# Gate and up products of a hybrid block: partial sums kept in PSUM banks and read out midway

## The chip, the cores and the metric

One core of a Trainium2 chip runs the whole kernel. The metric is device time in microseconds (us); the figure for the kernel before is the median of three runs. TensorE (PE in the rows) multiplies into PSUM, which has eight banks of 128 partitions by 512 float32 values here; VectorE (DVE), ScalarE (ACT) and GpSimd (POOL) work beside it, and SyncE (SP) issues the DMAs. Each engine takes its instructions strictly in the order in which they stand, and waits on semaphores for the others.

## What is computed

One layer on 2048 tokens of width 1024 in float32: a norm, an input projection, two mixers (gated linear attention and spatial gating), an output projection, then the feed-forward part with 2816 hidden columns, and a final norm. The change touches the two products `a` and `bu` of the feed-forward part alone:

```python
n2 = rms_norm(h, norm2_w[l])
a = jnp.einsum('btd,df->btf', n2, w_ffn_gate[l])
bu = jnp.einsum('btd,df->btf', n2, w_ffn_up[l])
h = h + jnp.einsum('btf,fd->btd', jax.nn.silu(a) * bu, w_ffn_down[l])
```

## The kernel before

The tokens go through in two halves of 1024 (`for s in range(2)`), each half as two blocks of 512. The gate and up products (`gate_up`) treat a half as 2 x 2 blocks: two blocks of tokens, two halves of D, two column tiles of 128. Winograd's form of Strassen's scheme makes the four result blocks of a pair of column tiles from seven block products instead of eight. There are 11 pairs in a half (i = 0 to 10), each with one `Weights` object for gate and then one for up: 22 objects, 154 block products per half. Pair 0 goes alternately between gate and up, since its token operands are still being made; from pair 1 on gate's seven products come first and then up's.

A block product m takes a weight operand `op` and a token operand `t1` to `t7`. Both are split into a high and a low part (`split`: ScalarE casts the high part, line 94, VectorE subtracts it for the low part, line 95), and `mm3` multiplies low by high, high by low and high by high: 3 matmuls for each of 4 tiles of K, so 12 of 128x512 a product, lines 114 to 116. `prep` makes the weight operands, seven products ahead (`AHEAD`), with sums of weight blocks by VectorE (`sw`, line 634).

Before, every product has a PSUM bank of its own (`o = ps()`; eight banks go round). The sums are made outside: products 1, 5 and 7 are copied out by ScalarE (line 659), and VectorE adds everything up, with eight additions for a `Weights` object: line 662 once, 666 once, 669 once, 672 once, and the one in `put_gate` (line 686) or `put_up` (line 692) four times. `put_gate` then applies Silu in place in the tile `cg` (line 687). `put_up` multiplies up's block into `cg` (line 693) and writes three of the four blocks to DRAM (`ad`, line 696). After the last block four more VectorE rows make the sums `cs` (lines 700 to 703) that the down-projection needs, which go to DRAM too (704, 705).

The tiles `cg`, `cs` and the 14 token operands all come from one pool of 16 buffers (`big`). So in gate and up two buffers are left for `cg` and `cs`, and a pair's `cg` lies where the `cg` of the pair before it lay: it can be written only after VectorE has read the old one for `cs` and after the three writes of line 696 have landed.

A scheduler sets the order in which each engine's instructions stand. The names below are tiles with the number that the build gave them; they differ between the two kernels only where the change made other tiles.

Of the kernel before, what the change touches and what calls it, by code (L numbers as in the profile page):

```python
# [15 lines left out]
P = 128  # L16
# [17 lines left out]
def hybrid_block(ctx, tc, x, norm1_w, w_in, w_gate_up, b_gate_up, gla_norm_w, sg_ln_w, sg_ln_b,  # L34
# [15 lines left out]
    def ps():  # L50
        return psp.tile([P, 512], F32, name="ps", tag="ps")
# [11 lines left out]
    # A generator emits one step at a time; tick() runs a step of each after a weight tile's products.  # L63
# [28 lines left out]
    def split(hi, lo, src):  # L92
        """hi + lo == src, each with 12 significant bits."""
        nc.scalar.copy(hi, src)  # L94
        nc.vector.tensor_tensor(lo, src, f32(hi), ALU.subtract)  # L95
# [5 lines left out]
    def load_w(srcs, a, b):  # L101
        """srcs: DRAM views [P, a, ...], side by side; the two parts of [P, a, b] in SBUF."""
        raw = view(rawp, F32, "raw", a, b)
        o = 0
        for s in srcs:
            nc.sync.dma_start(raw[:, :, o:o + s.shape[2]], s)
            o += s.shape[2]
        hi, lo = view(wp, F32R, "whi", a, b), view(wp, F32R, "wlo", a, b)
        split(hi, lo, raw)
        return hi, lo  # L110

    def mm3(o, l, r, first, last):
        (lh, ll), (rh, rl) = l, r
        nc.tensor.matmul(o, lhsT=ll, rhs=rh, start=first, stop=False)  # L114
        nc.tensor.matmul(o, lhsT=lh, rhs=rl, start=False, stop=False)  # L115
        nc.tensor.matmul(o, lhsT=lh, rhs=rh, start=False, stop=last)  # L116

    def rsq(dst, ss, n, k):
        """dst = 1 / sqrt(ss / n + eps)"""
        nc.vector.tensor_scalar(dst, ss, 1.0 / n, EPS, ALU.mult, ALU.add)  # L120
        nc.gpsimd.tensor_tensor(dst, dst, half[:, :k], ALU.pow)
# [8 lines left out]
    class Act:  # L130
        """A transposed operand: nk row tiles of 128 by 512 tokens, two parts."""
# [10 lines left out]
        def row(self, k, n=1):  # L142
            """Row tiles k .. k+n-1, for all tokens."""
            s = slice(k % 4, k % 4 + n)
            return self.hi[k // 4][:, s, :], self.lo[k // 4][:, s, :]

        def put(self, i, t, src):
            """Row tiles 4i .. 4i+3 of token tile t from PSUM."""
            s = slice(t * P, (t + 1) * P)
            split(self.hi[i][:, :, s], self.lo[i][:, :, s], src.rearrange("p (a b) -> p a b", b=P))  # L150

    def row_tiles(u):
        """Two units as four row tiles of D."""
        return [u[t // 2].rearrange("p a b -> p (a b)")[:, (t % 2) * D:(t % 2 + 1) * D] for t in range(TT)]
# [36 lines left out]
    def tok_group(w, col_list, act, ks=2, order=None, outer=None, done=None, before=None, ws=None, hook=None, pre=None):  # L191
        """Token-major product: four PSUM tiles [128 tokens, n]."""
        n = sum(c for _, c in col_list)
        order = order or list(range(0, act.nk, ks))
        acc = [None] * TT

        def load(k0):
            return tok_load(w, col_list, k0, min(ks, act.nk - k0))

        def products(t, k0, hi, lo):  # L200
            if acc[t] is None:
                acc[t] = ps()
            for j in range(hi.shape[1]):
                mm3(acc[t][:, :n], act(k0 + j, t * P, (t + 1) * P), (hi[:, j, :], lo[:, j, :]),
                    k0 == order[0] and j == 0, k0 == order[-1] and j == hi.shape[1] - 1)

        if outer:
            ws = ws or [load(k0) for k0 in order]
            for ts in outer:
                for k0, (hi, lo) in zip(order, ws):  # L210
                    if hook:
                        hook(ts[-1], k0)
                    for t in ts:
                        products(t, k0, hi, lo)
                for t in ts:
                    done(t, acc[t])
                tick()
        else:
            for k0 in order:
                if before and k0 in before:  # L220
                    finish(before[k0])
                hi, lo = pre.pop(k0) if pre and k0 in pre else load(k0)
                for t in range(TT):
                    products(t, k0, hi, lo)
                    if k0 == order[-1]:
                        done(t, acc[t])
                tick()
# [4 lines left out]
    def col_pair(ws, act, a=0, b=NB):  # L232
        """Transposed product: two PSUM tiles [128 columns, tokens a..b]."""
        acc = [ps(), ps()]
        for i, (hi, lo) in enumerate(ws):
            for k in range(4):
                for c in range(2):
                    cs = slice(c * P, (c + 1) * P)
                    mm3(acc[c][:, :b - a], (hi[:, k, cs], lo[:, k, cs]), act(4 * i + k, a, b), i + k == 0, i == 1 and k == 3)
            tick()  # L240
        return acc
# [15 lines left out]
    # 0 where a chunk starts, 1 elsewhere: the prefix scan's carry  # L257
# [3 lines left out]
    # keep[j, i] = 1 where j <= i, in both halves of the rows  # L261
# [12 lines left out]
    # the decay's up-projection: rows hi, hi, lo against the low-rank input's hi, lo, hi  # L274
# [9 lines left out]
    def constants():  # L284
# [9 lines left out]
        # spatial gating: masked, transposed weights and the two biases  # L294
# [27 lines left out]
    def down_sums():  # L322
        """The four sums of blocks of w_d that the down-projection takes, to DRAM."""
# [18 lines left out]
    def mix(blk, nT, first_w):  # L342
        """Both mixers of one block; the transposed operand of the output projection."""
# [59 lines left out]
        # The two factors of a head's output: its queries and scores, its state and values. Of the 128 rows,  # L403
        # the head's own half (as its keys lie) holds the former, the other half the latter.
# [3 lines left out]
        def right(n):  # L408
            """[rows, head in pair, pair, DV] of chunk n"""
            return rights[n % 2][:, n // 2]  # L410
# [169 lines left out]
    def project(blk, hx, mixT, g_att, pre, put, outer, ahead=None):  # L580
        """Output projection, residual, norm 2."""
# [28 lines left out]
    # Blocks: column tile c, half of D, half of the tokens. An operand m is the m-th factor's two parts.  # L610
    ORDER = (1, 2, 5, 7, 6, 3, 4)
    AHEAD = 6

    class Weights:
        """One pair of column tiles of w, as seven operands; put(c, l, in0, in1, tmp) takes a result's two addends."""

        def __init__(self, w, c0, act, put, tmp, unit=False):
# [9 lines left out]
            self.act, self.put, self.tmp, self.op, self.t = act, put, tmp, {}, {}  # L627

# [21 lines left out]

        def mul(self, m):
            o = ps()
# [22 lines left out]
    def gate_up(s, act):  # L675
        def matrices(i):
            unit = []

# [5 lines left out]
            def put_gate(c, l, x, y, tmp):  # L684
                g = part(2 * c + l)
                nc.vector.tensor_tensor(g, x, y, ALU.add)
                nc.scalar.activation(g, g, AF.Silu)

            def put_up(c, l, x, y, tmp):
                g = part(2 * c + l)  # L690
                u = tpt("u") if tmp is None else tmp
                nc.vector.tensor_tensor(u, x, y, ALU.add)
# [4 lines left out]
                if (c, l) == (1, 0):  # L697
# [12 lines left out]
            def tmp_up(m):  # L710
                return tpt(f"p{m}")

            return [lambda: Weights(w_g, 2 * i * P, act, put_gate, tmp_gate),
                    lambda: Weights(w_u, 2 * i * P, act, put_up, tmp_up, i == 0)]

        seq = []
        for i in range(NF // 2):
            mats = matrices(i)
            if i == 0:
                seq += [(2 * i + j, mats[j], m) for m in ORDER for j in range(2)]  # L720
            else:
                seq += [(2 * i + j, mats[j], m) for j in range(2) for m in ORDER]
# [3 lines left out]
        def ahead(n):  # L726
            """Operands up to the n-th product."""
# [7 lines left out]
        def run(late):  # L735
            for at, (key, _, m) in enumerate(seq):
# [9 lines left out]
    # Blocks: half of the tokens, column tile of a pair, half of D.  # L746
# [129 lines left out]
    for s in range(2):  # L876
# [118 lines left out]
```

## Time and profile before

| | us |
|---|---|
| median of three runs | 2015.6 (2015.26 to 2017.57) |
| span of the profiled execution | 2014.3 |
| TensorE busy | 1987.2 (99%) |
| VectorE busy | 1422.5 (71%) |
| ScalarE busy | 858.8 (43%) |

The span is 1.3 us under the median; what lies around the span of the profiled execution is not listed. Gate and up lie at about 382 to 803 us in the first half and at 1375 to 1796 us in the second, some 421 us each. Mean clock of TensorE over the span: 0.998 of full speed. A matmul's row gives 389 ns, but matmuls overlap: the starts of two that follow each other are 0.227 us apart, which is what counts.

### The profile page before, as it was taken

The numbers are of one execution on the slowest core, as the hardware profiler recorded it, in microseconds if no ns is written. First come the engines' busy times: TensorE is split into PE (matmuls) and PEld (weight loads), VectorE is DVE, ScalarE is ACT, GpSimd is POOL, SyncE is SP. The second block draws the span as 40 slices with busy tenths as digits, with TensorE's granted clock in tenths as the row PEclk, the third lists the DMA queues.
The fourth block names the chain that finished last, engine by engine and source line by source line (L and its number), as shares of the span: only waits on it lengthen the run. The fifth ranks groups of instructions, "written<-read, shape, count | busy, mean of one in ns | idle before, by whom it ended". The sixth has DMA issues, their size and how long they took to land. (4 is left out here: it accounts for less than half of the span.)

```text
span 2014.3 us, 26324 instructions
## 1 busy us (share of the span) xinstructions
PE 1987.2 (99%) x9909; PEld 1659.1 (82%) x9909; DVE 1422.5 (71%) x2397; ACT 858.8 (43%) x1418; POOL 80.8 (4%) x102
## 2 busy tenths in 40 slices
PE   7999999999999999999999999999999999999998
PEld 6888888878888888888888888887888888888886
DVE  5676776798777777555776655658977877775466
ACT  4534635453333333433562535346433333334334
POOL 1011000000000000000100100100000000000000
PEclk9999999999999999999999999999999999999999
DMA  5646664323323324865754344323332332367555
GB/s 192 188 168 222 228 200 167 115 94 105 115 95 102 118 95 145 290 200 185 242 178 105 115 143 144 103 84 116 114 111 95 106 114 95 104 208 268 188 164 197
DMA packets 189790, 303.05 MB, mean 150 GB/s; under 512 B 14503, under 2 KB 93021, under 8 KB 188638
## 3 DMA queue, kind: packets, MB, share of 16 engines
q1 hardware_dynamic: 189662, 301.36, 45.2%
q8 instruction: 78, 1.28, 0.3%
q14 instruction: 50, 0.41, 0.1%
HBM read 224.25 MB, written 72.88 MB: 148 GB/s over the span
## 5 line engine op out<-in xcount | busy, mean ns | idle before, releaser
L94 ACT CAST whi<-raw 128x1024 fp32r<-128x1024 f32 (+3 forms) x191 | 192.0, 1006 | 403.3 <-PE ps L115 208.5
L95 DVE TENSOR_TENSOR wlo<-raw,whi 128x1024 fp32r<-128x1024 f32 (+3 forms) x191 | 221.9, 1168 | 150.1 <-ACT whi L94 144.1
L114 PE MATMUL ps<-whi,aop 128*128 128x512 f32 x552 | 215.1, 390 | 0.0
L116 PE MATMUL ps<-whi,aop 128*128 128x512 f32 x552 | 214.8, 389 | 0.0
L115 PE MATMUL ps<-wlo,aop 128*128 128x512 f32 x552 | 214.8, 389 | 0.0
L94 ACT CAST op<-sw 128x512 fp32r<-128x512 f32 x176 | 107.5, 621 | 184.5 <-DVE sw L634 159.6
L114 PE MATMUL ps<-whi,nTl 128*128 128x512 f32 (+2 forms) x512 | 177.4, 346 | 3.4 <-DVE nTl L95 3.4
L116 PE MATMUL ps<-whi,nTh 128*128 128x512 f32 (+2 forms) x512 | 174.4, 341 | 0.0
L115 PE MATMUL ps<-wlo,nTh 128*128 128x512 f32 (+2 forms) x512 | 174.3, 340 | 0.0
L95 DVE TENSOR_TENSOR aop<-raw,aop 128x1024 fp32r<-128x1024 f32 x84 | 95.3, 1135 | 97.5 <-ACT aop L94 97.3
L95 DVE TENSOR_TENSOR op<-sw,op 128x512 fp32r<-128x512 f32 x176 | 121.5, 692 | 43.0 <-ACT op L94 42.6
L94 ACT CAST aop<-raw 128x1024 fp32r<-128x1024 f32 x84 | 82.0, 979 | 136.6 <-DMA raw<-ad 135.1
L116 PEld LDWEIGHTS ps<-whi,aop 128*128 128x128 f32 x552 | 103.6, 188 | 21.6
L115 PEld LDWEIGHTS ps<-wlo,aop 128*128 128x128 f32 x552 | 103.6, 188 | 21.4
L114 PEld LDWEIGHTS ps<-whi,aop 128*128 128x128 f32 x552 | 103.6, 188 | 21.4
L659 ACT COPY p<-ps 128x512 f32<-128x512 f32 x88 | 51.5, 588 | 149.2 <-PE ps L116 143.6
L95 DVE TENSOR_TENSOR op<-raw,op 128x512 fp32r<-128x512 f32 x132 | 89.3, 693 | 31.0 <-ACT op L94 30.5
L114 PEld LDWEIGHTS ps<-whi,nTl 128*128 128x128 f32 x512 | 98.1, 192 | 14.5 <-ACT whi L94 3.5
L116 PEld LDWEIGHTS ps<-whi,nTh 128*128 128x128 f32 x512 | 98.1, 192 | 10.2
L115 PEld LDWEIGHTS ps<-wlo,nTh 128*128 128x128 f32 x512 | 98.2, 192 | 9.4
L114 PE MATMUL ps<-whi,mixTl 128*128 128x512 f32 x256 | 101.9, 398 | 1.4 <-DVE mixTl L95 1.2
L114 PE MATMUL ps<-nTh,wlo 128*128 128x512 f32 x256 | 101.8, 398 | 0.0
(229 smaller groups left out, 4712.4 us busy)
## 6 DMA issues: line engine op xcount, KB each, us to landing
raw<-in_w_in_dram SPq DMA_DIRECT2D x72, 512.0 KB, 3.9
raw<-ad SPq DMA_DIRECT2D x70, 512.0 KB, 3.9
raw<-in_w_ffn_gate_dram SPq DMA_DIRECT2D x44, 512.0 KB, 3.6
raw<-in_w_ffn_up_dram SPq DMA_DIRECT2D x44, 512.0 KB, 3.6
raw<-td SPq DMA_DIRECT2D x40, 512.0 KB, 3.9
ad<-cg SPq DMA_DIRECT2D x66, 256.0 KB, 2.0
ad<-cs SPq DMA_DIRECT2D x22, 768.0 KB, 3.6
raw<-in_w_out_dram SPq DMA_DIRECT2D x32, 512.0 KB, 3.8
```

Of the source, the lines that this page charges most:

```text
L94: nc.scalar.copy(hi, src)
L95: nc.vector.tensor_tensor(lo, src, f32(hi), ALU.subtract)
L114: nc.tensor.matmul(o, lhsT=ll, rhs=rh, start=first, stop=False)
L115: nc.tensor.matmul(o, lhsT=lh, rhs=rl, start=False, stop=False)
L116: nc.tensor.matmul(o, lhsT=lh, rhs=rh, start=False, stop=last)
L659: nc.scalar.copy(t[m], o)
```

## The change

For the pairs 1 to 10 (`if i:`) `Weights` gets a function `keep`, and `mul` goes to the new `mul_kept`. An object then takes three banks instead of seven: products 1, 6, 5 and 3 are added up in the first, 7 and 4 in the second, 2 has the third (`BANK`). A product that is not the first in its bank starts without clearing it. The products go in the order 1, 2, 6, 7, 5, 4, 3 (`MULTIPLIED`), their operands are made in the order 1, 2, 5, 6, 7, 4, 3 (`PREPARED`). The bank's running sum is read in the middle: ScalarE copies it after products 1, 6 and 7; VectorE reads it after 5 and after 4 and adds one of the copies; after 3 it is the result block (0, 1) as it stands. Of the eight additions three are left. Gate's copies go straight into `cg` (parts 0, 2, 3), and gate's block (0, 1) goes from PSUM through Silu into `cg`. Block (1, 0) is now written out before (0, 1), and `cs` follows (0, 1). Pair 0 is left as it was.

```diff
-        nc.tensor.matmul(o, lhsT=ll, rhs=rh, start=first, stop=False)
+        nc.tensor.matmul(o, lhsT=ll, rhs=rh, start=first, stop=False, skip_group_check=shared)
...
+    PREPARED, MULTIPLIED = (1, 2, 5, 6, 7, 4, 3), (1, 2, 6, 7, 5, 4, 3)
+    BANK = {1: 0, 6: 0, 5: 0, 3: 0, 7: 1, 4: 1, 2: 2}
...
+        def mul_kept(self, m):
+            key = BANK[m]
+            first = key not in self.acc
+            if first:
+                self.acc[key] = ps()
+            o = self.acc[key]
+            (wh, wl), (th, tl) = self.op.pop(m), self.act[m]
+            for k in range(4):
+                mm3(o, (wh[:, k], wl[:, k]), (th[:, k], tl[:, k]), first and k == 0, k == 3, True)
+            t = self.t
+            if m in (1, 6, 7):
+                t[m] = self.keep(m)
+                nc.scalar.copy(t[m], o)
+            elif m == 3:
+                self.put(0, 1, o, None, None)
+            else:
+                c, l, other = {2: (0, 0, 1), 5: (1, 1, 7), 4: (1, 0, 6)}[m]
+                self.put(c, l, o, t[other], t[other])
...
             def put_gate(c, l, x, y, tmp):
                 g = part(2 * c + l)
+                if y is None:
+                    nc.scalar.activation(g, x, AF.Silu)
+                    return
...
-                if (c, l) == (1, 0):
+                left.discard((c, l))
+                if not left:
                     cs = bigt(F32, "cs")
...
+            if i:
+                def keep_gate(m):
+                    return part({1: 0, 6: 2, 7: 3}[m])
+
+                def keep_up(m):
+                    return tpt(f"p{m}")
...
-                seq += [(2 * i + j, mats[j], m) for j in range(2) for m in ORDER]
+                seq += [(2 * i + j, mats[j], m) for j in range(2) for m in PREPARED]
+                muls += [(2 * i + j, m) for j in range(2) for m in MULTIPLIED]
```

TensorE, the gate products of pair 1 in the first half. Before, the first row of each product; `ps_` is its bank's tile, `t1h` the token operand, and the semaphore named after "waits" belongs to VectorE (DVE) or ScalarE (Activation):

```order
L114 MATMUL ps_3963<-t1h_3308,op_3831 128x512 [waits DVE_49]
...
L114 MATMUL ps_3985<-t2h_3352,op_3850 128x512 [waits DVE_49]
...
L114 MATMUL ps_4004<-t5h_3495,op_3872 128x512 [waits DVE_49]
...
L114 MATMUL ps_4023<-t7h_3663,op_3893 128x512 [waits DVE_49]
...
L114 MATMUL ps_4043<-t6h_3697,op_3913 128x512 [waits DVE_49]
```

In the change, at the same place:

```order
L115 MATMUL ps_3963<-t1h_3308,op_3831 128x512 [waits DVE_49]
...
L115 MATMUL ps_3985<-t2h_3352,op_3850 128x512 [waits DVE_49]
...
L115 MATMUL ps_4021<-t7h_3663,op_3913 128x512 [waits DVE_49]
...
L115 MATMUL ps_3963<-t6h_3697,op_3892 128x512 [waits Activation_49]
...
L115 MATMUL ps_4021<-t4h_3760,op_3932 128x512 [waits DVE_49,Activation_49]
...
L115 MATMUL ps_3963<-t5h_3495,op_3872 128x512 [waits Activation_49]
...
L115 MATMUL ps_3963<-t3h_3728,op_3960 128x512 [waits DVE_49]
```

Here the scheduler has put 7 ahead of 6, and 5 after the first four matmuls of 4; in the other 19 objects of a half the order is that of `MULTIPLIED`. Product 6 comes back to the bank of product 1 and waits for ScalarE's copy out of it, product 5 for the copy after 6.

ScalarE at the same place. Before, from the casts of up's operands to the first copy into pair 1's `cg` (`cg_3998`); DMAHW is a DMA queue's semaphore:

```order
L687 ACTIVATE cg_3690<-cg_3690 128x512 [waits DVE_49]
L94 CAST op_3982<-raw_3978 128x512 [waits DMAHW6_49,Activation_49]
L94 CAST op_4001<-raw_3979 128x512 [waits DMAHW0_49,Activation_49]
L659 COPY cg_3998<-ps_4004 128x512 [waits DMAHW5_49,DMAHW1_49,DMAHW7_49,DVE_49,PE_49]
L659 COPY cg_3998<-ps_4023 128x512 [waits PE_49]
```

In the change, where pair 1's `cg` is `cg_3976`:

```order
L718 ACTIVATE cg_3690<-cg_3690 128x512 [waits DVE_49]
L94 CAST op_3960<-sw_3870 128x512 [waits DVE_49,PE_49,Activation_49]
L94 CAST op_3982<-raw_3978 128x512 [waits DMAHW6_49,PE_49,Activation_49]
L669 COPY cg_3976<-ps_3963 128x512 [waits DMAHW5_49,DMAHW7_49,DMAHW1_49,PE_49]
L94 CAST op_4000<-raw_3979 128x512 [waits DMAHW0_49,Activation_49]
L94 CAST op_4018<-sw_4016 128x512 [waits DVE_49,PE_49,Activation_49]
L669 COPY cg_3976<-ps_4021 128x512 [waits PE_49]
L718 ACTIVATE cg_3976<-cg_3976 128x512 [waits DVE_49]
L94 CAST op_4036<-sw_4016 128x512 [waits DVE_49,Activation_49]
L669 COPY cg_3976<-ps_3963 128x512 [waits PE_49]
```

The first copy into the new `cg` was that of product 5 and is now that of product 1; it waits for the same three writes of pair 0's `cg`.

VectorE at the turn from a later pair to the next. Before, from up's last product (`ps_4518`, product 4) on:

```order
L672 TENSOR_TENSOR p7_4468<-p7_4468,ps_4518 128x512 [waits PE_49]
L700 TENSOR_TENSOR cs_4535<-cg_4289 128x512 [waits DMAHW4_49,DMAHW3_49,DVE_49]
...
L701 TENSOR_TENSOR cs_4535<-cs_4535,cg_4289 128x512 [waits DVE_49]
...
L702 TENSOR_TENSOR cs_4535<-cg_4289 128x512
L703 TENSOR_TENSOR cs_4535<-cg_4289,cs_4535 128x512 [waits DVE_49]
```

In the change, from up's product 4 (`ps_4422`) over its last, 3 (`ps_4362`), to the first addition of the next gate:

```order
L726 TENSOR_TENSOR p6_4415<-ps_4422,p6_4415 128x512 [waits PE_49]
L95 TENSOR_TENSOR op_4500<-sw_4417,op_4500 128x512 [waits Activation_49]
L727 TENSOR_TENSOR cg_4246<-p6_4415,cg_4246 128x512 [waits DVE_49]
L727 TENSOR_TENSOR cg_4246<-ps_4362,cg_4246 128x512 [waits PE_49]
L95 TENSOR_TENSOR op_4522<-raw_4518,op_4522 128x512 [waits Activation_49]
L735 TENSOR_TENSOR cs_4492<-cg_4246 128x512 [waits DMAHW5_49,DMAHW4_49,DVE_49]
L737 TENSOR_TENSOR cs_4492<-cg_4246 128x512
L736 TENSOR_TENSOR cs_4492<-cs_4492,cg_4246 128x512 [waits DVE_49]
L738 TENSOR_TENSOR cs_4492<-cg_4246,cs_4492 128x512 [waits DVE_49]
```

The four `cs` rows now come in one piece, two rows behind the block of the last product; ScalarE's first copy of the next gate waits for the last of them.

## Rows read from the trace of the kernel before

**Rows 1.** Part 1 of the page: busy us of each engine, share, instructions.

```profile
PE 1987.2 (99%) x9909; PEld 1659.1 (82%) x9909; DVE 1422.5 (71%) x2397; ACT 858.8 (43%) x1418; POOL 80.8 (4%) x102
```

**Rows 2.** Busy time by stretch: PE, PEld, DVE, ACT, POOL; then clock, DMA, GB/s.

```profile
400.00:450.00 50.00, 48.43 (x214) 39.76 (x213) 49.82 (x84) 27.04 (x49) 0.00 (x0) 1.00 0.27 89
450.00:500.00 50.00, 50.00 (x222) 41.40 (x221) 40.08 (x65) 18.73 (x32) 0.00 (x0) 1.00 0.34 111
700.00:750.00 50.00, 50.00 (x222) 41.39 (x221) 37.03 (x58) 19.27 (x34) 0.00 (x0) 1.00 0.31 100
```

**Rows 3.** What PE waited for, whole span, down to 1 us: total, times, longest.

```profile
PE ps L166 <- DVE xsu L159: 9.8, 1, 9.8
PE ps L114 <- DVE nTl L95: 3.4, 2, 3.2
PE ps L115 <- ACT op L94: 3.1, 2, 1.6
PE ps L453 <- DVE right L462: 1.2, 3, 0.4
PE ps L114 <- DVE mixTl L95: 1.2, 1, 1.2
...
```

**Rows 4.** Groups of instructions by line: busy us, mean ns, idle before and releasers.

```profile
L94 ACT CAST op<-sw 128x512 fp32r<-128x512 f32 x176 | 107.5, 621 | 184.5 <-DVE sw L634 159.6 <-PE ps L116 24.9
L659 ACT COPY p<-ps 128x512 f32<-128x512 f32 x88 | 51.5, 588 | 149.2 <-PE ps L116 143.6 <-DVE cg L686 4.6
L692 DVE TENSOR_TENSOR p<-p,p 128x512 f32<-128x512 f32 x66 | 45.6, 690 | 0.1
```

**Rows 5.** Timeline of PE, first half: start us, us, line, tiles [idle before].

```profile
412.05 0.47 PE L115 MATMUL ps<-t3l,op 128*128 128x512 f32 x1 [1.57 <-ACT op L94]
...
422.82 0.39 PE L114 MATMUL ps<-t1h,op 128*128 128x512 f32 x1
...
430.98 0.39 PE L114 MATMUL ps<-t7h,op 128*128 128x512 f32 x1
...
444.58 0.39 PE L114 MATMUL ps<-t2h,op 128*128 128x512 f32 x1
```

**Rows 6.** Timeline of VectorE, first half, from pair 0 into pair 1.

```profile
428.63 0.72 DVE L95 TENSOR_TENSOR op<-sw,op 128x512 fp32r<-128x512 f32 x1
...
434.04 0.72 DVE L693 TENSOR_TENSOR cg<-p,cg 128x512 f32<-128x512 f32 x1
...
435.84 0.73 DVE L703 TENSOR_TENSOR cs<-cg,cs 128x512 f32<-128x512 f32 x1
```

**Rows 7.** Timeline of ScalarE, first half.

```profile
436.93 1.07 ACT L659 COPY cg<-ps 128x512 f32<-128x512 f32 x2 [2.99 <-PE ps L116]
...
444.78 0.59 ACT L659 COPY p<-ps 128x512 f32<-128x512 f32 x1 [0.29 <-PE ps L116]
```

**Rows 8.** The write of pair 0's last block: its issue, and landing by line (KB, us).

```profile
434.79 0.34 SPq L696 DMA_DIRECT2D ad<-cg  x1
...
ad<-cg SPq DMA_DIRECT2D x66, 256.0 KB, 2.0
```

**Rows 9.** The same place in the second half: PE, VectorE, ScalarE.

```profile
1415.64 0.39 PE L114 MATMUL ps<-t1h,op 128*128 128x512 f32 x1
...
1426.84 0.72 DVE L693 TENSOR_TENSOR cg<-p,cg 128x512 f32<-128x512 f32 x1
...
1429.74 1.08 ACT L659 COPY cg<-ps 128x512 f32<-128x512 f32 x2 [3.00 <-PE ps L116]
```

**Rows 10.** Busy time by stretch, columns as in rows 2: TensorE's granted clock.

```profile
20.00:25.00 5.00, 5.00 (x42) 5.00 (x42) 2.17 (x12) 2.12 (x5) 2.19 (x3) 1.00 0.91 322
34.00:37.00 3.00, 3.00 (x15) 3.00 (x15) 0.76 (x4) 1.05 (x1) 0.00 (x0) 0.50 0.00 0
409.00:413.00 4.00, 2.43 (x11) 1.75 (x10) 4.00 (x7) 1.67 (x4) 0.00 (x0) 1.00 0.06 23
2008.00:2011.00 3.00, 0.00 (x0) 0.00 (x0) 1.51 (x4) 0.67 (x2) 0.55 (x1) 0.83 0.00 0
```

More of the change, by code (lines that the diff above doesn't have):

```diff
@@ L110, in load_w, with mm3 @@
         return hi, lo
-    def mm3(o, l, r, first, last):
+    def mm3(o, l, r, first, last, shared=False):
         (lh, ll), (rh, rl) = l, r
-        nc.tensor.matmul(o, lhsT=ll, rhs=rh, start=first, stop=False)
-        nc.tensor.matmul(o, lhsT=lh, rhs=rl, start=False, stop=False)
-        nc.tensor.matmul(o, lhsT=lh, rhs=rh, start=False, stop=last)
+        nc.tensor.matmul(o, lhsT=ll, rhs=rh, start=first, stop=False, skip_group_check=shared)
+        nc.tensor.matmul(o, lhsT=lh, rhs=rl, start=False, stop=False, skip_group_check=shared)
+        nc.tensor.matmul(o, lhsT=lh, rhs=rh, start=False, stop=last, skip_group_check=shared)
     def rsq(dst, ss, n, k):
@@ L611, in hybrid_block, with __init__ @@
     ORDER = (1, 2, 5, 7, 6, 3, 4)
+    PREPARED, MULTIPLIED = (1, 2, 5, 6, 7, 4, 3), (1, 2, 6, 7, 5, 4, 3)
+    BANK = {1: 0, 6: 0, 5: 0, 3: 0, 7: 1, 4: 1, 2: 2}
     AHEAD = 6
     class Weights:
-        def __init__(self, w, c0, act, put, tmp, unit=False):
+        def __init__(self, w, c0, act, put, tmp, unit=False, keep=None):
             srcs = [w[k0 * P:(k0 + 4) * P, c0:c0 + 2 * P].rearrange("(k p) c -> p k c", p=P) for k0 in (0, 4)]
@@ L627, in __init__ @@
             self.act, self.put, self.tmp, self.op, self.t = act, put, tmp, {}, {}
+            self.keep, self.acc = keep, {}
         def prep(self, m):
@@ L649, in prep @@
             self.op[m] = o[:, 0], o[:, 1]
+        def mul_kept(self, m):
[16 more added lines that the diff above has]
+                self.put(c, l, o, t[other], t[other])
         def mul(self, m):
+            if self.keep:
+                return self.mul_kept(m)
             o = ps()
@@ L677, in matrices @@
             unit = []
+            left = {(c, l) for c in range(2) for l in range(2)}
             def part(k):
@@ L690, in put_up @@
                 g = part(2 * c + l)
-                u = tpt("u") if tmp is None else tmp
-                nc.vector.tensor_tensor(u, x, y, ALU.add)
+                if y is None:
+                    u = x
+                else:
+                    u = tpt("u") if tmp is None else tmp
+                    nc.vector.tensor_tensor(u, x, y, ALU.add)
                 nc.vector.tensor_tensor(g, u, g, ALU.mult)
@@ L711, in tmp_up @@
                 return tpt(f"p{m}")
-            return [lambda: Weights(w_g, 2 * i * P, act, put_gate, tmp_gate),
-                    lambda: Weights(w_u, 2 * i * P, act, put_up, tmp_up, i == 0)]
-        seq = []
+            keep_gate = keep_up = None
+            if i:
[3 more added lines that the diff above has]
+                    return tpt(f"p{m}")
+            return [lambda: Weights(w_g, 2 * i * P, act, put_gate, tmp_gate, keep=keep_gate),
+                    lambda: Weights(w_u, 2 * i * P, act, put_up, tmp_up, i == 0, keep=keep_up)]
+        seq, muls = [], []
         for i in range(NF // 2):
@@ L720, in gate_up @@
                 seq += [(2 * i + j, mats[j], m) for m in ORDER for j in range(2)]
+                muls += [(2 * i + j, m) for m in ORDER for j in range(2)]
             else:
-                seq += [(2 * i + j, mats[j], m) for j in range(2) for m in ORDER]
+                seq += [(2 * i + j, mats[j], m) for j in range(2) for m in PREPARED]
+                muls += [(2 * i + j, m) for j in range(2) for m in MULTIPLIED]
         made, preps = {}, iter(seq)
@@ L735, in run @@
         def run(late):
-            for at, (key, _, m) in enumerate(seq):
+            for at, (key, m) in enumerate(muls):
                 ahead(at + AHEAD + 1)
```

## Prediction

> **What bounds the kernel now.** I read the engine totals first: TensorE is busy 1987.2 of 2014.3 us and nothing else comes near, VectorE being next with 1422.5 [rows 1]. Shares are averages, so the stretches of gate and up come next: in each of them TensorE is busy all of its 50 us at a clock of 1.00, while VectorE has 10 to 13 us free, except between 400 and 450, where it is busy 49.82 [rows 2]. That is pair 0 and the turn to pair 1. The list of what TensorE waited for names no read-out of PSUM; from gate and up it has one line, 3.1 us in two waits for a cast [rows 3], and the timeline shows the first of them at 412.05 in pair 0 [rows 5]. So gate and up last as long as their matmuls. Less work on VectorE or ScalarE buys nothing here; a new wait of TensorE costs its full length.
>
> **The change, part by part.** The matmuls are the same in number and shape: 0.
>
> *Additions that go.* Five per object, 20 objects in a half, two halves: 200 rows of VectorE, at the 0.69 us of such an addition [rows 4] 138 us. VectorE falls to about 1284 us. None of it was on the path [rows 2, 3], so the gain is 0. ScalarE's copies and Silus keep their number.
>
> *New waits in the steady state.* A product that returns to a bank which is read out in the middle must wait for that reading: four times an object, 160 times in all. Between the product read and the one that waits lies one other product of 12 matmuls, 2.72 us at 0.227 each. What a reading takes shows where before copies a product out: the next product starts at 444.58 [rows 5], the copy at 444.78 and lasts 0.59 [rows 7]. With 0.1 us to TensorE, my allowance for the signal, that is 0.9 of 2.72, so 1.8 us are to spare. The tightest place is the turn to the next pair, where gate's first copy goes into `cg` behind the four `cs` rows. From the end T of up's product 3, VectorE has six rows to do. Its rows start 0.60 apart (434.04 to 435.84 is three of them) and finish 0.72 after their start [rows 6]: 0.25 + 5 x 0.60 + 0.72 = T + 4.0. The copy then ends at about 4.7, TensorE may start at 4.8, and product 6 is due after two products, at T + 5.44. Slack 0.6 us, at 18 turns (pairs 2 to 10, two halves). I take 0 and keep the place for a rival.
>
> *The turn from pair 0 to pair 1.* Here the same copy comes at the worst moment. In gate's pair 1 the order on TensorE is 1, 2, 7, 6, part of 4, 5, rest of 4, 3. Product 1 starts at 422.82 and the fourth product is due at 430.98 [rows 5]. Now the fourth is 6, which needs product 1 copied into the new `cg`; the buffer still holds pair 0's `cg`. Its last block is multiplied at 434.04 [rows 6], its write is issued at 434.79 and such a write takes 2.0 us [rows 8]: 436.8. The trace shows this wait already: ScalarE's first copy into the new `cg`, idle 2.99 us ahead, starts at 436.93 [rows 7], although the releaser named, TensorE, had long been done with that product (the third, over at 430.98). Before, it hid, because the product had a bank that nobody wanted back. On ScalarE the copy also stands behind two casts, the first of which waits for a sum that VectorE makes one row behind the last `cs` row. One row, the low part now earlier, has left the queue ahead, so this sum takes the place of the row at 435.84 and ends at 436.6 [rows 6]. Two casts of 0.62 [rows 4] follow, a little overlapped, and the copy runs from 437.7 to 438.3, and TensorE starts product 6 at 438.4: 438.4 - 430.98 = 7.4 us late. A smaller wait lies inside: product 7 comes third, at 428.26 (422.82 + 2 x 2.72), but its low part is the row at 428.63 [rows 6], so it starts at about 429.45 and ends at 432.17. TensorE then idles from 432.17 to 438.4, 6.2 us. What stands behind the waiting copy on ScalarE are casts for products that come later still, and Silus.
>
> Next late is product 5. It wants the copy made after 6, and that stands behind a cast of a sum eight VectorE rows on: 435.84 + 8 x 0.60 = 440.64, done 441.4; cast 0.62, copy 0.59 [rows 4], so TensorE may go at 442.7. Product 6 ends at 441.1, four matmuls of 4 at 442.0: 0.7 us more.
>
> *The clock.* After a stop of 1.57 us the granted clock stayed at 1.00 (409 to 413); in a stretch without any matmul at the end of the kernel it fell to 0.83 [rows 10], so 6.2 us of idleness probably cost it. A stretch at 0.50, the lower level of 1.2 GHz, is seen early in the kernel: 15 matmuls in 3 us, where at 1.00 five us held 42, so 25 in three [rows 10]. Ten of 25 lost is 1.2 us; I take one such stretch of 3 us, and twice it as the upper end. Product 6 would then end at about 442.3, and the 0.7 us for product 5 vanish in that. So 7.4 + 1.2 = 8.6 us a half, or 8.1 if the clock holds.
>
> One more sentence on the clock, which the sum doesn't need: the Trainium skill, TensorE: Matmul & The Clock Gate, section "HAM oscillation — how this bites in real kernels", says that idle gaps between dense stretches of matmuls bring the slow clock back each time; the stop at 412 shows that not every gap does, no row here shows one of 6 us between matmuls, and by the rule the figure is 8.6, without it 8.1.
>
> *Second half.* The same rows stand there: product 1 at 1415.64, the last block at 1426.84, the copy into `cg` at 1429.74 [rows 9]. From product 1 to the copy it is 14.10 us there and 436.93 - 422.82 = 14.11 here. So the same 8.6.
>
> *Sum.* 2 x 8.6 = 17.2 us onto the profiled execution's 2014.3 gives a span of 2031.5. The median stands 1.3 over that span: 2032.8. Lower end: only the landing counts, 436.8 + 0.59 + 0.1 - 430.98 = 6.5 a half, 2028.6. Upper end: 8.1 and twice 1.2, 10.5 a half, 2036.6.
>
> **Rivals.** *R1, faster or no change: the copy doesn't wait.* If the buffer of `cg` were free by 430, as it would be if the first copy went elsewhere or the writes landed some 6.5 us sooner, only product 7's 1.2 us a half would be left: 2015.6 + 2.4 = 2018.0. Without that too, 2015.6; and if the 3.1 us of [rows 3] went with the lighter VectorE, 2012.5. For it: VectorE has less to do in all. Against it: the 200 additions go from pair 1 on, while pair 0, which delays the writes, keeps all of its own; and the copy at 436.93 [rows 7] shows the landing.
>
> A rule bears on this. The list of TensorE's waits has no line for a read-out [rows 3]. The Trainium skill, PSUM — Partial Sum Buffer, section "PSUM bank collisions raise a hardware error", says that no two engines may touch one bank at once and that semaphores must guard it bank by bank; so with three banks for seven products the read-outs enter TensorE's path. By the row read alone the time stays 2015.6, by the rule it is the forecast. No run here shows which yet.
>
> *R2, slower still: later turns wait too.* The slack of 0.6 us at 18 turns rests on six VectorE rows running without a hitch. If VectorE gets there 1.2 us late, two rows of 0.60, each turn costs 0.6: 18 x 0.6 = 10.8, together 2043.6. For it: the `cs` rows stand in one piece right ahead. Against it: VectorE is idle a quarter of the time there [rows 2], less loaded still after the change, and a row or two may also run sooner.
>
> *R3, the clock holds.* 2 x 8.1 = 16.2: 2031.8. It is the forecast but for 1 us, and counted with it.
>
> **How the numbers follow.** The turn at pair 1 stalls and nothing else does (R3 included): 0.80, own range 2028.6 to 2036.6. R2: 0.11. R1: 0.06, of which 0.02 come out faster and 0.04 within 0.2% of 2015.6 (4 us, about what a measurement of this kernel can tell from no change). Anything else, on the slower side: 0.03. The predicted time is 2032.8. The range runs from 2028.0, the lower end, to 2041.0, which takes in R2 where half of its turns wait (2032.8 + 5.4) and some more of the clock. Faster 0.02, same 0.04, slower 0.94.
>
> **What would show it.** In the profile of the changed kernel, TensorE's list of waits should have a new line: for ScalarE's copy into `cg`, about 6.2 us, twice, some 1000 us apart; in the timeline product 6 of pair 1 at about 438.4, with the copy at 437.7 behind two casts. The stretches around 440 should show a granted clock under 1.00, those of 450 to 800 TensorE busy all the time and no such wait. VectorE's total should be near 1284 us in 2197 rows. I am wrong if product 6 starts by 433 (R1: the copy had another release), if waits for copies turn up at every pair (R2), or if the gap is there and the time isn't longer, which would mean that TensorE was not the bound.

## The result, and the profile of the changed kernel

The change makes the kernel slower: 2038.8 us (median of 4 runs, 2037.0 to 2044.1) against 2016.6 before (4 runs), ratio 1.0113, 95% interval 1.0099 to 1.0128. In a second set of runs it was 2036.3 against 2015.7, ratio 1.0097 (1.0081 to 1.0113). The forecast was 2032.8 in a range of 2028 to 2041.

The page first, busy us of each engine, to be held against [rows 1]:

```profile
PE 1991.8 (98%) x9909; PEld 1659.7 (82%) x9909; DVE 1308.8 (64%) x2197; ACT 860.6 (42%) x1418; POOL 81.8 (4%) x102
```

The 200 additions are gone, and VectorE works 114 us less. TensorE does the same 9909 instructions in a span of 2035.2 us. What it waited for, over the whole span (total, times, longest), against [rows 3]:

```profile
PE ps L115 <- ACT cg L669: 11.9, 2, 5.9
PE ps L167 <- DVE st L121: 9.7, 1, 9.7
PE ps L115 <- DVE nTl L95: 3.4, 2, 3.2
PE ps L116 <- ACT op L94: 3.1, 2, 1.6
PE ps L115 <- DVE op L95: 1.9, 2, 1.0
PE ps L116 <- DVE bop L95: 1.6, 2, 0.9
```

The first line is new and the largest: two waits for the copy of line 669, the first one of gate's pair 1. The fifth is new too, product 7's low part at the same place. The last belongs to the end of the down-projections; more of it below.

The turn from pair 0 to pair 1 on TensorE, first and second half, against [rows 5] and [rows 9] (start, us, line, tiles, idle ahead; the first matmul of a product each):

```profile
420.09 0.39 PE L115 MATMUL ps<-t1h,op 128*128 128x512 f32 x1
...
426.66 0.50 PE L115 MATMUL ps<-t7h,op 128*128 128x512 f32 x1 [0.97 <-DVE op L95]
...
435.60 0.79 PE L115 MATMUL ps<-t6h,op 128*128 128x512 f32 x1 [5.93 <-ACT cg L669]
...
440.88 0.44 PE L115 MATMUL ps<-t4h,op 128*128 128x512 f32 x1
...
441.85 0.41 PE L115 MATMUL ps<-t5h,op 128*128 128x512 f32 x1
...
1423.87 0.39 PE L115 MATMUL ps<-t1h,op 128*128 128x512 f32 x1
...
1430.44 0.50 PE L115 MATMUL ps<-t7h,op 128*128 128x512 f32 x1 [0.97 <-DVE op L95]
...
1439.39 0.79 PE L115 MATMUL ps<-t6h,op 128*128 128x512 f32 x1 [5.92 <-ACT cg L669]
```

Everything here lies 2.7 us earlier than before, a difference that arose in the first 40 us of the kernel, which the change doesn't touch. By the starts 1.5 us of it come from the stretch where the profiled execution before had a clock of 0.50 ([rows 10], 34 to 37); in the change's the clock was 1.00 there:

```profile
33.00:36.00 3.00, 3.00 (x25) 2.98 (x24) 1.64 (x4) 2.05 (x3) 0.00 (x0) 1.00 0.00 0
```

So times are counted from product 1. Product 6 is due 3 x 2.72 = 8.16 us after it, at 428.25, and starts at 435.60: 7.35 us late. It then takes 440.88 - 435.60 = 5.28 us instead of 2.72.

ScalarE, VectorE and SyncE at the same place, against [rows 6 to 8]; the last line is the time from issue to landing of such a write within 425 to 440:

```profile
433.93 0.62 ACT L94 CAST op<-sw 128x512 fp32r<-128x512 f32 x1 [4.25 <-DVE sw L640]
434.45 0.61 ACT L94 CAST op<-raw 128x512 fp32r<-128x512 f32 x1
434.97 0.58 ACT L669 COPY cg<-ps 128x512 f32<-128x512 f32 x1
...
431.34 0.67 DVE L727 TENSOR_TENSOR cg<-p,cg 128x512 f32<-128x512 f32 x1
...
433.14 0.67 DVE L640 TENSOR_TENSOR sw<-raw,sw 128x512 f32<-128x512 f32 x1
...
432.04 0.34 SPq L730 DMA_DIRECT2D ad<-cg  x1
...
ad<-cg SPq DMA_DIRECT2D x1, 256.0 KB, 2.1
```

VectorE finishes the last block of pair 0 and its `cs` rows, then the sum at 433.14. ScalarE stands idle 4.25 us for that sum, does two casts, and only then the copy. The write landed at about 432.04 + 2.1 = 434.1, some 0.8 us before the copy began: the casts ended last.

TensorE's clock around it (columns as in [rows 2]), and a stretch of the later pairs:

```profile
431.00:434.00 3.00, 0.00 (x0) 0.00 (x0) 3.00 (x6) 0.07 (x1) 0.00 (x0) 1.00 0.38 137
434.00:437.00 3.00, 1.40 (x3) 1.16 (x4) 3.00 (x6) 3.00 (x7) 0.00 (x0) 0.52 1.02 322
437.00:440.00 3.00, 3.00 (x8) 2.31 (x7) 2.23 (x4) 1.22 (x3) 0.00 (x0) 0.50 0.49 157
440.00:443.00 3.00, 3.00 (x12) 2.32 (x11) 1.57 (x3) 1.11 (x2) 0.00 (x0) 0.84 0.59 170
443.00:446.00 3.00, 3.00 (x15) 2.46 (x14) 1.18 (x2) 1.08 (x2) 0.00 (x0) 1.00 0.00 0
...
450.00:500.00 50.00, 50.00 (x222) 41.40 (x222) 29.31 (x45) 18.29 (x32) 0.00 (x0) 1.00 0.27 85
```

The clock fell during the stop (1.00 from 431 to 434, 0.52 from 434 to 437, and product 6 starts at 435.60). It is 0.50, its lower level of 1.2 GHz, through the whole of product 6: 8 matmuls in three us, where the line from 443 has 15. From 443 on all is as before, and from 450 TensorE is busy without a gap.

Where the 20.9 us between the two profiled spans lie follows from the starts of the same matmuls in both traces (after minus before):

| at | shift, us | gained since |
|---|---|---|
| product 1 of gate's pair 1, first half | -2.73 | -2.7 (first 40 us) |
| product 1 of gate's pair 2, first half | +7.29 | **+10.0** |
| product 1 of gate's pair 1, second half | +8.23 | +0.9 |
| product 1 of gate's pair 2, second half | +18.13 | **+9.9** |
| first matmul of the second down-projection | +18.13 | 0.0 |
| last matmul | +20.86 | +2.7 |

The two turns are 19.9 us, nearly all of it. The pairs 2 to 10 cost nothing.

### The profile page after: what moved, and what is told of

It is laid out like the page before. It is cut to its first block, busy times and chain, and to the rows that moved or that the text cites. A ratio compares the mean times of both kernels' runs of the same rounds, so it can differ in the third digit from the quotient of the medians.

```text
span 2035.2 us, 26141 instructions
## 1 busy us (share of the span) xinstructions
PE 1991.8 (98%) x9909; PEld 1659.7 (82%) x9909; DVE 1308.8 (64%) x2197; ACT 860.6 (42%) x1418; POOL 81.8 (4%) x102
## 5 line engine op out<-in xcount | busy, mean ns | idle before, releaser
L94 ACT CAST op<-raw 128x512 fp32r<-128x512 f32 x132 | 81.2, 621 | 130.1 <-PE ps L117 129.5
L116 PEld LDWEIGHTS ps<-wlo,aop 128*128 128x128 f32 x552 | 103.6, 188 | 22.2 <-DVE wlo L95 0.9
L117 PEld LDWEIGHTS ps<-whi,nTh 128*128 128x128 f32 x512 | 96.9, 189 | 10.2
```

The costliest lines, as they stand in the source:

```text
L117: nc.tensor.matmul(o, lhsT=lh, rhs=rh, start=False, stop=last, skip_group_check=shared)
```

## Experiments

**Only from pair 2 on.** Pair 1 stays as before:

```diff
-            if i:
+            if i > 1:
                 def keep_gate(m):
...
+            elif i == 1:
+                seq += [(2 * i + j, mats[j], m) for j in range(2) for m in ORDER]
+                muls += [(2 * i + j, m) for j in range(2) for m in ORDER]
```

> Sums are kept in PSUM from pair 2 on; pair 1 stays as before. Turn theory (the whole loss lies where pair 0 goes over into pair 1, 10.0 us a half): the loss goes, 2016 us to within 3, and no wait of TensorE for a copy of line 669. Spread rival (what costs is the return to a bank anywhere, so it goes with the number of kept objects, 36 of 40): 2016.6 + 0.9 x 22.2 = 2036.6 us.

Measured: 2017.0 us (11 runs) against 2015.4 (21 runs), ratio 1.0003 (0.9994 to 1.0012). No wait for line 669 is left, and from pair 1 to pair 2 nothing is lost in either half (0.0 us by the starts). 36 of the 40 objects keep their sums in PSUM here, and it costs nothing that can be measured; nor does it gain anything.

**Only in pair 1.** The reverse, pairs 2 to 10 as before:

```diff
-            if i:
+            if i == 1:
                 def keep_gate(m):
...
+            elif i > 1:
+                seq += [(2 * i + j, mats[j], m) for j in range(2) for m in ORDER]
+                muls += [(2 * i + j, m) for j in range(2) for m in ORDER]
```

> Sums are kept in PSUM in pair 1 alone, pairs 2 to 10 stay as before. Turn theory: the loss is all there, 2036 to 2040 us, two waits of 5.9 us for the copy of line 669. Spread rival (4 of 40 kept objects): 2016.6 + 0.1 x 22.2 = 2018.8 us.

Measured: 2035.8 us, ratio 1.0098 (1.0084 to 1.0112). The turns cost 10.1 and 10.2 us. TensorE's timeline, product 6 of pair 1:

```profile
435.68 0.80 PE L115 MATMUL ps<-t6h,op 128*128 128x512 f32 x1 [5.89 <-ACT cg L669]
```

So the loss is in pair 1, whole; the spread rival is out.

**Copies aside.** In pair 1 gate's three copies go into small tiles:

```diff
-                    return part({1: 0, 6: 2, 7: 3}[m])
+                    return tpt(f"p{m}") if i == 1 else part({1: 0, 6: 2, 7: 3}[m])
```

> As the change, but in pair 1 gate's three copies go into small tiles of their own and not into cg, so the first copy needn't wait for pair 0's cg. Theory of the buffer (the copy waits for the old cg and for the casts that the scheduler put ahead of it for that reason): product 6 starts when it is due and both stalls go, 2016 us to within 3. Rival (the copy is late because VectorE and ScalarE are behind with pair 0, whatever its buffer): product 6 still waits several us, 2028 to 2038 us.

Measured: 2018.1 us (11 runs), ratio 1.0014 (1.0005 to 1.0023). TensorE's and ScalarE's timelines at the turn:

```profile
420.87 0.39 PE L115 MATMUL ps<-t1h,op 128*128 128x512 f32 x1
...
426.33 0.47 PE L115 MATMUL ps<-t6h,op 128*128 128x512 f32 x1
...
425.02 0.58 ACT L669 COPY p<-ps 128x512 f32<-128x512 f32 x1
```

Without the old `cg` in its way the scheduler puts the copy ahead of the casts of pair 1, it runs at 425.02, and product 6, now third, starts 5.46 us after product 1, when it is due (5.44). VectorE and ScalarE are as far behind with pair 0 as in the change, so it is the buffer, with the place in ScalarE's queue that follows from it. The two were not taken apart; an estimate from the change's rows is that the landing alone (434.1, then 0.59 for the copy and 0.1) would have made product 6 some 6.5 us late, and the casts added the rest of the 7.35. By the starts 0.6 us a half remain at the turn, in the products behind 6.

**Work in the gap.** 24 matmuls into a bank that nobody reads, ahead of product 7 of gate's pair 1:

```diff
+            if self.warm and m == 6:
+                d, x = ps(), self.act[1][0]
+                for k in range(self.warm):
+                    nc.tensor.matmul(d, lhsT=x[:, k % 4, :P], rhs=x[:, k % 4], start=k == 0, stop=k == self.warm - 1)
...
-            return [lambda: Weights(w_g, 2 * i * P, act, put_gate, tmp_gate, keep=keep_gate),
+            return [lambda: Weights(w_g, 2 * i * P, act, put_gate, tmp_gate, keep=keep_gate, warm=24 if i == 1 else 0),
```

The code asks for them with product 6; the scheduler put them ahead of 7, from 5.44 us after product 1 on.

> As the change, but in each half TensorE gets 24 more matmuls ahead of product 7 of gate's pair 1 (5.4 us of work into a bank that nobody reads), inside the idle stretch. Clock theory (of the 10.0 us a turn, 7.35 are the wait and 2.65 the lower clock behind it): product 6 starts at the same moment but runs at the full clock, 2038.8 - 2 x 2.65 = 2033.5 us. Rival (product 6 lasts 5.3 us because something else is late, operands or the bank): 2038.8 us; and if the added matmuls delay anything, more.

Measured: 2035.6 us, ratio 1.0099 (1.0086 to 1.0113), so 2 us more than expected. The added work still left a stop ahead of product 6, in both halves; its rows, that of the product behind (4), and the stretch behind each stop:

```profile
436.52 0.50 PE L115 MATMUL ps<-t6h,op 128*128 128x512 f32 x1 [1.77 <-ACT cg L673]
...
439.39 0.39 PE L115 MATMUL ps<-t4h,op 128*128 128x512 f32 x1
...
1438.53 0.50 PE L115 MATMUL ps<-t6h,op 128*128 128x512 f32 x1 [1.80 <-ACT cg L673]
...
1442.98 0.40 PE L115 MATMUL ps<-t4h,op 128*128 128x512 f32 x1
...
437.00:440.00 3.00, 3.00 (x15) 2.45 (x14) 2.63 (x5) 1.94 (x4) 0.00 (x0) 1.00 0.70 214
1439.00:1442.00 3.00, 3.00 (x10) 2.33 (x9) 2.65 (x5) 1.53 (x3) 0.00 (x0) 0.56 0.70 215
```

In the first half the clock stayed at 1.00, product 6 took 2.87 us and the turn cost 7.6. In the second, behind a stop of the same length, the clock was 0.56, product 6 took 4.45 us and the turn cost 9.2. Product 6 starts as late in both (15.5 us after product 1) and has the same operands; only the clock differs. So the long product 6 was the clock.

**The change again, and the gap closed.** 32 matmuls in place of 24, beside the change itself:

> The change itself once more, beside the runs below: 2037 to 2040 us. In the first pair of runs the stops, with the lower clock behind them, gave 20 us of the 22; the rest (waits of TensorE for bop near the end, 2.3 us) is small and should differ from run to run, not be there in the same size.

> As the change, with 32 added matmuls ahead of product 7 of gate's pair 1 in each half and not 24: 7.3 us of work, so that no stop of TensorE is left there. Clock theory (with 24 a stop of 1.8 us was left, and the clock fell behind it in one half of two): clock at 1.00 in both halves, 7.4 to 7.6 us a turn, 2015.4 + 15 = 2030.5 us, up to 2 more from the waits at the end. Rival (the clock has little to do with it): 2035 to 2038 us as with 24, with a slower product 6 though nothing stops.

Measured: the change 2036.3 us (5 runs), its turns 9.9 and 9.8 us; with the gap closed 2036.2 us, ratio 1.0096 (1.0081 to 1.0110). The trace did what the clock theory said, the median did not. Clock in the stretches of product 6, first and second half:

```profile
437.00:440.00 3.00, 3.00 (x14) 2.18 (x13) 3.00 (x6) 2.41 (x5) 0.00 (x0) 1.00 1.03 363
1442.00:1445.00 3.00, 3.00 (x14) 2.18 (x13) 3.00 (x6) 3.00 (x7) 0.00 (x0) 1.00 0.98 322
```

The turns cost 7.6 us each. But the profiled run lost 2.1 us at the end of the first down-projection, in waits like this one:

```profile
1003.96 0.47 PE L115 MATMUL ps<-whi,aop 128*128 128x512 f32 x1 [1.30 <-DVE aop L95]
```

The same step with pairs 2 to 10 as before:

> Sums kept in pair 1 alone, with the 32 added matmuls ahead of product 7 of gate there, so that nothing stops. Of the turn's 10.1 us in the run with pair 1 alone, 7.6 should stay and the lower clock's 2.5 should go: 2035.8 - 5.0 = 2030.8 us, with the clock at 1.00 in both halves. With all pairs kept the same step brought nothing in the median, as its profile lost 2.1 us at the end of the first half's down-projection; pairs 2 to 10 as before should have no such waits. Rival (what the clock costs is made up elsewhere in any case): 2035 to 2036 us.

Measured: 2032.9 us, ratio 1.0086 (1.0071 to 1.0101), against 1.0098 for pair 1 alone. Both turns cost 7.6 us, 2.5 less than the 10.1 and 10.2 there. Of the 5 us expected some 3 show in the median, and its interval holds both; the fastest two of the five runs took 2030.5 and 2031.0 us, and the profiled one was the slowest, 2036.7. In its profile the waits at the ends of the down-projections were there all the same (2.0 and 2.5 us), though pairs 2 to 10 were the old ones. So the new late pairs are not what makes these waits. They come to 0.3 us or less in the profiles of before, of pair 1 alone and of two versions below, and to 1.8 to 4.5 us in the others, with old late pairs and with new ones. Both profiles without the change are among the small ones, but so are two with it. Whether the change favours these waits, what sets them, and whether they give back part of what a turn gains, stays open.

**The margin of the later turns.** VectorE writes the last `cs` sum three times, in the version that keeps sums from pair 2 on:

```diff
-                    nc.vector.tensor_tensor(cs[:, 3], a12, cs[:, 1], ALU.subtract)
+                    for _ in range(3 if i > 1 else 1):
+                        nc.vector.tensor_tensor(cs[:, 3], a12, cs[:, 1], ALU.subtract)
```

> As the version that keeps sums from pair 2 on, but VectorE writes the last of the four cs sums three times in these pairs: two rows more ahead of gate's first copy into the next cg. In the change that copy starts 4.16 us after the end of up's last product and leaves TensorE 0.69 us, at 18 turns. Margin theory: with two rows more and one that the scheduler has put between, 3 x 0.60, the copy ends at about 6.7 and TensorE, due at 5.44, waits 1.3 to 1.4 us at each of 16 turns: 2017.0 + 22 = 2039 us. Rival (the rows are hidden, the margin is larger than it looks): 2017 to 2020 us.

Measured: 2020.9 us, ratio 1.0018 (1.0009 to 1.0027). By the starts it lost 1.4 and 1.6 us in the two halves, 0.2 a turn, not 1.4. TensorE and ScalarE at one such turn:

```profile
496.69 0.39 PE L115 MATMUL ps<-t1h,op 128*128 128x512 f32 x1
...
502.13 0.39 PE L115 MATMUL ps<-t7h,op 128*128 128x512 f32 x1
...
503.53 0.50 PE L115 MATMUL ps<-t6h,op 128*128 128x512 f32 x1
...
502.90 0.58 ACT L669 COPY cg<-ps 128x512 f32<-128x512 f32 x1
```

The copy came as late as the margin theory had it: it ends at 503.48, 6.79 us after product 1 (expected: 6.7), and product 6 starts at 6.84 and not at 5.44. But the scheduler saw the longer way and put six matmuls of product 7 (1.36 us) ahead of product 6, so TensorE had work meanwhile. So the margin is as small as it looked, and two rows use it up; what that costs where no other product is at hand was not measured.

**Pair 0 too.** In addition to the copies aside, pair 0 adds 6 onto 1 and 4 onto 7 in PSUM:

```diff
-            o = ps()
+            key = {6: 1, 4: 7}.get(m, m)
+            first = key == m
+            if first:
+                self.acc[key] = ps()
+            o = self.acc[key]
...
-                nc.vector.tensor_tensor(t[1], t[1], o, ALU.add)
+                nc.scalar.copy(t[1], o)
...
-                nc.vector.tensor_tensor(t[7], t[7], o, ALU.add)
-                self.put(1, 0, t[7], t[1], t[7])
+                self.put(1, 0, o, t[1], t[1])
```

> As the version with gate's copies aside in pair 1, and pair 0 too keeps two sums in PSUM: 6 is added onto 1 and 4 onto 7, so VectorE has two additions less an object there (four rows of 0.60 a half), ScalarE a copy more. VectorE is busy all the time in pair 0, and TensorE waits there 1.57 us a half. Theory (those waits, and the 0.8 us that product 6 still waits in pair 1 with the copies aside, come from VectorE's rows): 1.2 us of the first and the second go, 2018.1 - 2 x 2.0 = 2014 us, just under the kernel before. Rival (ScalarE's copies and the return to the bank in pair 0 cost as much): 2016 to 2020 us.

Measured: 2017.2 us (12 runs), ratio 1.0009 (1.0000 to 1.0017). That lies in the rival's range. The smaller part of the theory came: at the turn nothing is lost any more (0.0 us by the starts, 0.6 with the copies aside alone; the expectation put that at product 6 and had it wrong). The larger part did not, and could not: the wait in pair 0 stays, because the rows saved come behind it. Before, VectorE makes the sum that the cast waits for at 410.60, and the four rows (lines 666 and 672) start between 419.62 and 431.63. The wait with pair 0 changed too:

```profile
410.19 0.47 PE L116 MATMUL ps<-t3l,op 128*128 128x512 f32 x1 [1.52 <-ACT op L94]
```

**That wait itself.** The kernel before, with the weight sums of pair 0's products 6 and 3 on GpSimd:

```diff
-                nc.vector.tensor_tensor(dst, x, y, op)
+                (nc.gpsimd if unit_sums else nc.vector).tensor_tensor(dst, x, y, op)
```

(`unit_sums` holds in pair 0 for products 6 and 3.)

> The kernel before, without the change, but the weight sums of products 6 and 3 of pair 0 are made by GpSimd and not by VectorE. TensorE waits there 1.57 us a half for a cast that waits for such a sum. If VectorE's queue is what holds the sum up, the waits go: 2015.7 - 3.1 = 2012.6 us. If GpSimd takes longer over a sum than VectorE's queue held it up, the waits stay or grow: 2016 to 2022 us.

Measured: 2021.7 us, ratio 1.0026 (1.0017 to 1.0035). The wait for the cast went and others took its place, for token operands that VectorE makes:

```profile
PE ps L115 <- DVE t3l L95: 1.8, 2, 0.9
PE ps L115 <- DVE t5l L95: 1.3, 2, 0.7
...
PE ps L115 <- DVE t6l L95: 1.2, 2, 0.6
```

The sums on GpSimd slowed the engine that they were to relieve: a VectorE row that started while such a sum ran took 1.45 to 1.8 us, where such rows take 0.7 before. A sum on GpSimd, the row of VectorE that started beside it, and that row before:

```profile
403.60 1.29 POOL L635 TENSOR_TENSOR sw<-raw,sw 128x512 f32<-128x512 f32 x1 [3.09 <-ACT cg L688]
...
403.99 1.45 DVE L95 TENSOR_TENSOR t6l<-b,t6h 128x512 fp32r<-128x512 f32 x1
...
402.17 0.70 DVE L95 TENSOR_TENSOR t6l<-b,t6h 128x512 fp32r<-128x512 f32 x1
```

There are four such rows in each half, together 3.7 us longer, and the four sums had saved VectorE 4 x 0.60 = 2.4. By the starts pair 0 lasts 1.7 and 1.9 us longer than before. The rest of the 5 us does not stand in the profile, which is of a fast run (2017.6).

No version here beats the kernel before. In those that avoid the stall, gate and up last as long as TensorE's matmuls to within 1.6 us a half.

## Why the prediction was right, and the step whose size was off

- *What bounds the kernel*: right. 114 us less of VectorE bought nothing, and by the starts each us of waiting of TensorE was paid in full. VectorE's saving was put at 138 and is 113.7: rows of 0.69 us start 0.60 apart when they follow each other, and busy time counts the overlap once. It lay off the path.
- *The steady state*: right, and close. At the tightest turn the prediction had VectorE done at T + 4.0, the copy from 4.1 and 0.6 us to spare. The copy starts 4.16 after product 1 of the next gate (468.19), at 472.35, ends at 472.94, and product 6 starts when due:

```profile
472.35 0.59 ACT L669 COPY cg<-ps 128x512 f32<-128x512 f32 x1 [0.57 <-DVE cs L738]
...
473.63 0.39 PE L115 MATMUL ps<-t6h,op 128*128 128x512 f32 x1
```

  That leaves 0.69, and so it is at all 18 turns, 0.5 to 0.7. The rival of later waits (R2) didn't come.
- *The turn at pair 1*: right in place, cause and length. Late by 7.35 us against 7.4, idle from product 7's end (429.38) for 6.2 us as worked out, product 7 started 6.57 after product 1 against 6.63, the second half the same. Two casts stood ahead of the copy, as the order had it. R1 fell with pair 1 alone: the copy did wait. Copies aside turned R1 into a kernel, and it gave nearly R1's time (2018.1 against 2018.0). That was in part luck: R1 counts 1.2 us a half for product 7, and what was lost was 0.6, in the products behind 6.
- *Product 5's 0.7 us*: right that it vanishes behind the slower product 6; 5 starts at 441.85, 0.97 after the four matmuls of 4 began, which at the full rate are 0.91.
- *The clock*: right that it falls, wrong in size, and this is the term that was off. The prediction took 1.2 us a half, with twice that as the end. Product 6 took 2.6 us longer than at the full rate (5.28 - 2.72); 2.4 of it is the clock, since behind the stop of 1.77 us, with the clock at 1.00, it took 2.87. Two things made the term small. Most comes from its length: I took one stretch of 3 us, while the clock was low for all of product 6, over 5 us; ten of 25 lost over 5.28 us would have been 2.1. And 15 of 25 overstates the speed a little: such a count takes in the matmuls that reach over the ends of the stretch, and the 15 matmuls of [rows 10] are of 128x272, while 12 of 128x512 took 5.28 us instead of 2.72, about half. With 2.6 the sum is 2 x (7.35 + 2.6) = 19.9 us, a median of 2035.5. The two sets of runs gave 22.2 and 20.6 over before; the rest is of the size of the waits at the ends of the down-projections, which are open.
- *The range*: the mechanism's own upper end was 2036.6, and the first measured median, 2038.8, lies over it (the second, 2036.3, does not). It fell inside the range because room above was kept mainly for R2, which didn't come; that part is luck.

The two rules weighed in the prediction: the Trainium skill, PSUM — Partial Sum Buffer, section "PSUM bank collisions raise a hardware error", wants the accesses of two engines to one bank kept apart by semaphores. The trace agrees: product 6 waited for ScalarE's copy out of its bank, 11.9 us in two waits. The Trainium skill, TensorE: Matmul & The Clock Gate, section "HAM oscillation — how this bites in real kernels", has the slow clock come back with idle gaps between dense matmuls. Here it did behind the stops of 6.2 us each time, behind those of 1.8 us once in two, and behind those of 1.57 us in pair 0 never.

## What to carry to other kernels

When sums move into PSUM banks, each read-out joins TensorE's path: ask of every one what stands ahead of it on the engine that reads, and which buffer it writes, above all where the old scheme goes over into the new. A copy that could be late for free before may be the first thing that TensorE waits for afterwards. And price a stop of TensorE at its length plus the slower matmuls behind it, from rows of the same matmul shape: here 7.4 us cost 10.

## What the runs showed of the hardware that was not expected

- A 128x512 matmul takes its turn every 0.227 us at the granted clock of 1.00 and every 0.43 at 0.50, 53% of the rate, while [rows 10] had suggested 60%. Two neighbours in product 6:

```profile
436.19 0.63 PE L116 MATMUL ps<-t6l,op 128*128 128x512 f32 x1
436.62 0.63 PE L117 MATMUL ps<-t6h,op 128*128 128x512 f32 x1
```

- Two stops of the same 1.8 us, in the same program at the same place of its two halves, had different clocks behind them: 1.00 and 0.56. Behind the second the clock did not fall at once: the first matmuls of product 6 still started 0.23 to 0.34 us apart (1438.53, 1438.87, 1439.10, 1439.33), the later ones 0.43. Before the first, as before the second, TensorE had worked without a gap for the 5.4 us of added matmuls and product 7. So what a short stop costs differs from one place to the next by 1.6 us without any change in the code.
- GpSimd and VectorE did not work freely side by side: the VectorE row that started while a 128x512 sum ran on GpSimd took 1.45 to 1.8 us instead of 0.7, at all eight places in the profile of the version with GpSimd.
